# More expert blocks among the queries, and gathered rows begun four units later: a two-block transformer kernel on one core

## The chip, the cores and the metric

The kernel runs on 1 core of one Trainium2 chip. The metric is the device time of one execution in microseconds (us). Three runs of the kernel before gave 2555.89, 2561.6 and 2565.39 us (median 2561.6). One further execution was profiled; all rows below come from it.

## The reference

Two transformer blocks over 512 tokens of width 1024 in float32. The change touches only the feed-forward part of the first block, a "PEER" layer that retrieves 16 of 16384 single-neuron experts for each of 8 heads:

```
q = (xc @ wq).reshape(chunk, 8, 2, 128)
s = einsum('chpd,hpkd->chpk', q, subkeys)          # scores against 2 x 128 subkeys
s1, i1 = top_k(s[:, :, 0], 16); s2, i2 = top_k(s[:, :, 1], 16)
cand = s1[..., :, None] + s2[..., None, :]         # 16 x 16 candidates
cs, ci = top_k(cand, 16); eidx = experts of ci; g = softmax(cs)
hid = einsum('cd,chkd->chk', xc, u_table[eidx])
a   = gelu(hid) * g
out = einsum('chk,chkd->cd', a, v_table[eidx])
```

Ahead of it stand the attention heads of the first block, behind it the whole second block (retention, convolution, gated feed-forward); neither is changed.

## The kernel before, in words

**Two ways to the same experts.** For the first 384 tokens (`GT`) the kernel does not gather: it multiplies all 16384 experts densely, 128 blocks of 128 experts, and spreads the retrieved weights into a dense table `gates`. For the last 128 tokens it gathers the 128 retrieved rows of `u_table` and then those of `v_table` by indirect DMA (`row`, 128 x 1024 floats, 0.524 MB each, 256 in all) and multiplies them on VectorE (`gather_step`: `scr`/`hg` for the u rows, `acc` for the v rows).

**Units.** The dense work is a list `self.order` of units. A "q" unit is one 128-column chunk of the query projection, a "u" unit the up-projection of one expert block (`up`, 24 matmuls, then a gelu into `gel`), a "v" unit the down-projection of one block (18 matmuls into the six banks `oacc`). Every unit needs one weight tile of 0.524 MB: loaded into `ws` four units ahead (`DEEP`) by SyncE's DMA queue, rounded to a high part `wh` on ScalarE two units ahead (`AHEAD`, `stage_high`), and its low part `wl = ws - wh` made two units ahead as well (`stage_low`), on VectorE or GpSimd. TensorE multiplies high x high, high x low and low x high. A v unit also needs `gel` times its gates (`stage_gate`, VectorE), the high part `ah` of that (ScalarE) and its low part `al` (`stage_al`, VectorE).

**Three stages.** `run_queries`: q units, with u units dealt between them. VectorE meanwhile takes the top 16 of each score chunk (`tv`, `ti`); after every fourth chunk, a group of two heads, it forms the candidates (`cand` on VectorE, `cidx` on GpSimd), their top 16 (`cv`, `ci`) and, in pieces dealt between the next group's top-16s, the expert numbers (`oh`, `ov`, `ef`). The stage's result is `iff`, the indices as floats. `run_gates`: TensorE transposes the indices (`it`) and multiplies one-hot tables (`o`) into `gates`, again with u units between; each finished 2 MB part of `gates` is written to DRAM by a DMA on ScalarE's queue. `run_experts`: the other u units and all v units alternate; after the last u, v units alone. `weight` deals the 256 gathered rows over this stage's units.

**What sets the order.** These stages are recorded by hand: each engine runs its instructions in the order in which the code emits them. `plan` makes the list of units from estimated costs (`V_TOP`, `V_OH`, ...: VectorE's time of each piece, `PE_U`, `PE_Q`: TensorE's): it puts u units after a q unit while the estimated backlog of VectorE (`wait`) is over `BACK`. A u block done before there is room keeps its gelu in DRAM and is read back later (`gel<-gel_d`). In `run_queries` every fourth low part and the last five are on VectorE, the others on GpSimd, and each is emitted at the head of its unit:

```
pool = s < self.nq - 5 and s % 4 < 3
self.stage_low(x, self.nc.gpsimd if pool else self.nc.vector)
x = self.at(s + 1) if s + 1 >= 0 else None
if x is not None and x["k"] == "v":
    self.stage_al(x)
```

In `run_experts` the order within a unit is: load, `wh`, gate and `ah`; the gather steps; then `lows`, that is the low part `wl` two units ahead and, last, `al` one unit ahead; then the unit's matmuls. `NROW = 6` row buffers are in flight.

Of the kernel before, what the change touches and what calls it, by code (L numbers as in the profile page):

```python
# [22 lines left out]
NTB = 4  # L23
# [17 lines left out]
NROW = 6  # L41
AHEAD = 2
DEEP = AHEAD + 2
USTEP = 1.6
NQ = 3

PE_Q, PE_U, PE_GP, PE_IT = 6.35, 4.17, 0.95, 2.1
V_TOP, V_CAND, V_TOPC, V_OH, V_OV, V_RED, V_Z, V_LOW, V_O, V_PREP = 1.68, 5.0, 1.3, 0.6, 0.9, 0.9, 0.8, 1.25, 2.85, 4.5
BACK = 8.0
CAND = [(a, 16 // (a + 1)) for a in range(16)]  # L50
NCAND = sum(n for _, n in CAND)
# [43 lines left out]
class Builder:  # L95
# [384 lines left out]
    def plan(self):  # L480

        self.order, self.events = [], []
        un, wait = 0, NQ * NTB * V_TOP
        for c in range(NQ, 16):
            self.order.append({"k": "q", "c": c})
            wait += NTB * V_TOP - PE_Q
            if c % 4 == 3:
                wait += V_CAND + 8 * (V_TOPC + V_OH + V_RED) + V_Z + (4 * V_OV if c == 15 else 0)  # L490
            while wait > (BACK if c < 15 else 0):
                self.order.append({"k": "u", "i": un})
                wait -= PE_U
                un += 1
        self.nq = len(self.order)
        pt, dt = 0.0, V_PREP

        def fill(t):
            nonlocal pt, dt, un
            while pt < t():  # L500
                self.events.append(("u", 0))
                self.order.append({"k": "u", "i": un})
                pt, dt, un = pt + PE_U, dt + V_LOW, un + 1

        fill(lambda: dt)
        self.events.append(("it", 0))
        pt += PE_IT
        dt = max(dt, pt + 1.5)
        for i in range(GT // 8):
            dt += V_O  # L510
            fill(lambda: dt)
            self.events.append(("gp", i))
            pt += PE_GP
        self.ng = len(self.order)
        self.far = far = un - (LEAD - ME - AHEAD - 1)
        units = []
        for j in range(-ME, 128):
            while un < 128 + far and un - far < min(128, j + LEAD - AHEAD - 1):
                i = un
                un += 1  # L520
                units.append({"k": "u" if i < 128 else "re", "i": i, "j": i - far})
                if i < 128:
                    break
            if j >= 0:
                units.append({"k": "v", "j": j})
        for x in self.order:
            if x["k"] == "u":
                x["j"] = x["i"] - far if x["i"] >= far else 128 - far + x["i"]
        for x in units:
            if x["k"] == "re":  # L530
                self.order[-1].setdefault("re", []).append(x)
            else:
                self.order.append(x)
# [121 lines left out]

    def run_queries(self, ps):

        self.sk, self.qc, self.tvs = {}, {}, {}
        self.todo, self.pieces = deque(), deque()
        for c in range(NQ):  # L660
            self.load_sk(c)
        for s in range(-DEEP, 0):
            self.ahead(s)
            self.lows(s)
        for c, p in enumerate(ps):
            self.take_q(c, p)
        for c in range(NQ - 1):
            self.scores(c)
        pt = dt = 0.0
        old = NQ - 1  # L670
        for s in range(self.nq):
            x = self.order[s]
            self.ahead(s)
            self.lows(s)
            if x["k"] == "q":
                p = self.mm("q")
                self.mul(p, x)
                self.take_q(x["c"], p)
                pt += PE_Q
            else:  # L680
                self.stage_up(x)
                self.stage_gelu(x)
                pt += PE_U
            if old is not None:
                self.scores(old)
            old = x["c"] if x["k"] == "q" else None
            while self.todo and (dt < pt or s == self.nq - 1):
                cost, f = self.todo.popleft()
                f()
                dt += cost  # L690
            if not self.todo:
                dt = max(dt, pt)

# [10 lines left out]
    def run_gates(self):  # L704

        nc = self.nc
# [15 lines left out]
        def turn():  # L722
            for j in range(3):
                p = self.bank("at", "it")
                for tb in range(ND):
                    src = iff[:, j, tb] if j < 2 else self.g[:, tb].rearrange("p h k -> p (h k)")
                    nc.tensor.transpose(p[:, tb * 128:tb * 128 + 128], src, self.ident)
                if j < 2:
                    nc.scalar.activation(iT[j], p[:, :GT], AF.Copy)
                else:  # L730
                    nc.scalar.activation(gT[0], p[:, :GT], AF.Copy, scale=GSCALE)
                    nc.vector.scalar_tensor_tensor(gT[1], p[:, :GT], GSCALE, gT[0], op0=OP.mult, op1=OP.subtract)

        def hots(i):
            if i >= GT // 8:
                return
            t0 = 8 * i
            o = os[i] = [self.tmp.tile([128, 4, 128, 2], FP16, tag=f"o{j}", bufs=1 if j == 1 else 3, name=f"o{j}")
                         for j in range(4)]
            io = self.iota2[:, None].to_broadcast([128, 4, 128, 2])  # L740

            def bc(x):
                x = x[:, t0:t0 + 8].rearrange("p (j s) -> p j s", s=2)
                return x[:, :, None, :].to_broadcast([128, 4, 128, 2])

            nc.vector.tensor_tensor(o[0], io, bc(iT[0]), OP.is_equal)
            nc.vector.tensor_tensor(o[1], io, bc(iT[1]), OP.is_equal)
            nc.vector.tensor_tensor(o[2], o[1], bc(gT[0]), OP.mult)
            nc.vector.tensor_tensor(o[3], o[1], bc(gT[1]), OP.mult)
# [14 lines left out]
            if q == GC // 8 - 1:  # L764
                nc.scalar.dma_start(self.gd[:, c], gs[0])

        s = self.nq
        for kind, i in self.events:
            if kind == "it":
                turn()  # L770
                hots(0)
                hots(1)
            elif kind == "gp":
                spread(i)
                hots(i + 2)
            else:
                x = self.order[s]
                self.ahead(s)
                self.lows(s)
                self.stage_up(x)  # L780
                self.stage_gelu(x)
                s += 1

    def ahead(self, s):

        x = self.at(s + DEEP)
        if x is not None:
            self.stage_load(x)
        x = self.at(s + AHEAD) if s + AHEAD >= 0 else None
        if x is not None:  # L790
            self.stage_high(x)
            if x["k"] == "v":
                self.stage_gate(x)

    def lows(self, s):

        x = self.at(s + AHEAD) if s + AHEAD >= 0 else None
        if x is not None:
            pool = s < self.nq - 5 and s % 4 < 3
            self.stage_low(x, self.nc.gpsimd if pool else self.nc.vector)  # L800
        x = self.at(s + 1) if s + 1 >= 0 else None
        if x is not None and x["k"] == "v":
            self.stage_al(x)

    def wtile(self, tag, dt):

# [69 lines left out]
    def run_experts(self):  # L876


        self.grs, self.wcount = {}, {}
        self.load_gates(0)  # L880
        weight = [USTEP if x["k"] == "u" else 1.0 for x in self.order]
        n = len(self.order)
        total, spent, done, issued, last = sum(weight[self.ng:]), 0.0, 0, 0, []
        for s in range(self.ng, n):
            self.ahead(s)
            spent += weight[s]
            while done < (256 if s == n - 1 else min(256, 256 * spent / total)):
                while issued < min(256, done + NROW):
                    self.issue_row(issued)
                    issued += 1  # L890
                self.gather_step(done)
                done += 1
            self.lows(s)
            x = self.order[s]
            if x["k"] == "u":
                self.stage_up(x)
                self.stage_gelu(x)
            else:
                y = (x["j"], x["ah"], x["al"], x["wh"], x["wl"])
                if x["j"] < 128 - VT:  # L900
                    for i in range(6):
                        self.vmul(i // 2, i % 2, *y)
                else:
                    last.append(y)
        return last
# [442 lines left out]
```

## Time and profile before

| | |
|---|---|
| median of 3 runs | 2561.6 us (2555.89 to 2565.39) |
| the profiled execution | 2559.39 us, its span 2557.6 us |
| TensorE busy | 2471.1 us (97%) |
| VectorE / ScalarE / GpSimd busy | 1721.6 / 940.7 / 601.5 us |
| DMA over the span | 494.24 MB, mean 193 GB/s |

The span is what the profiler saw from the first to the last instruction; the execution takes 1.8 us more. Busy shares are means over stages with different limits, so each stage has to be read by itself. In a row of a timeline the bracket at the end is the idle time of that engine just before the instruction, and what ended it. PE is TensorE, DVE VectorE, ACT ScalarE, POOL GpSimd, SP SyncE; "q" behind a name is its DMA queue.

### The profile page before, as it was taken

What the parts mean: (1) busy time and instruction counts of PE and PEld (TensorE: products, weight loads), DVE (VectorE), ACT (ScalarE), POOL (GpSimd) and SP (SyncE); (2) the same over time, 40 slices, a digit from 0 to 9 for tenths busy, and PEclk for the clock granted to TensorE, in tenths of its full rate; (3) what the DMA queues carried; (4) which work ended last, traced back from release to release, by engine and by line L of the source; (5) the groups of instructions that cost most, each with busy time, mean ns of one, the idle gap of its engine ahead of it and who ended that gap; (6) DMA issues with size and microseconds to landing.
All of it is one profiled execution on the core that took longest, in us unless ns stands there. A gap on an engine that the chain in (4) does not pass through costs nothing.

```text
span 2557.6 us, 34104 instructions
## 1 busy us (share of the span) xinstructions
PE 2471.1 (97%) x12867; PEld 2138.2 (84%) x12867; DVE 1721.6 (67%) x3226; ACT 940.7 (37%) x1401; POOL 601.5 (24%) x455
## 2 busy tenths in 40 slices
PE   8999999997998999999999999999999999999998
PEld 6788898887997899999988787777888888888887
DVE  5767568999896788888887897777644335433323
ACT  4666343343553333333333333521232223422221
POOL 1132146541003455545443351100000001000000
PEclk9999999998998999999999999999999999999999
DMA  4476244334768999999999995422222223222332
GB/s 154 143 246 218 71 132 136 117 127 135 285 238 309 357 339 340 327 337 340 333 362 361 346 377 175 161 80 86 83 99 99 93 97 108 75 95 95 95 99 62
DMA packets 188693, 494.24 MB, mean 193 GB/s; under 512 B 15848, under 2 KB 83304, under 8 KB 186992
## 3 DMA queue, kind: packets, MB, share of 16 engines
q1 hardware_dynamic: 140768, 320.64, 37.2%
q0 software_dynamic: 36864, 134.23, 14.5%
q10 hardware_dynamic: 10896, 37.18, 3.9%
q8 instruction: 101, 1.65, 0.3%
q14 instruction: 64, 0.52, 0.1%
HBM read 454.10 MB, written 37.90 MB: 192 GB/s over the span
## 4 chain that ended last, share of the span: by engine, by line
PE 75%; DVE 12%; DMA 6%; ACT 3%; issue 3%; POOL 1%; SPq 0%; ACTq 0%; DVEq 0%; POOLq 0%
PE up L146 5%; PE up L148 5%; PE up L147 5%; DMA ws<-in_v_blk 5%; PE oacc L914 4%; PE oacc L913 4%; PE oacc L912 4%; PE fg L147 2%; PE fg L148 2%; PE fg L146 2%; PE fd L146 2%; PE fd L147 2%; PE fd L148 2%; PE fu L147 1%; PE fu L148 1%
## 5 line engine op out<-in xcount | busy, mean ns | idle before, releaser
L140 ACT ACTIVATE wh<-ws 128x1024 fp32r<-128x1024 f32 (+1 forms) x204 | 214.3, 1051 | 664.4 <-issue 233.7
L141 DVE TENSOR_TENSOR wl<-ws,wh 128x1024 fp32r<-128x1024 f32 (+1 forms) x198 | 240.5, 1215 | 255.0 <-ACT wh L140 253.6
L840 DVE TENSOR_TENSOR wl<-ws,wh 128x1024 fp32r<-128x1024 f32 x236 | 290.6, 1232 | 163.4 <-ACT wh L836 158.8
L836 ACT ACTIVATE wh<-ws 128x1024 fp32r<-128x1024 f32 x269 | 284.1, 1056 | 206.4 <-DMA ws<-in_v_blk 132.3
L148 PE MATMUL up<-xh,wl 128*128 128x384 f32 x1024 | 346.1, 338 | 12.4 <-DVE wl L840 11.7
L146 PE MATMUL up<-xh,wh 128*128 128x384 f32 x1024 | 348.2, 340 | 0.0
L147 PE MATMUL up<-xl,wh 128*128 128x384 f32 x1024 | 344.3, 336 | 0.0
L914 PE MATMUL oacc<-wh,al 128*128 128x512 f32 x768 | 302.7, 394 | 9.9 <-DVE al L856 9.8
L913 PE MATMUL oacc<-wl,ah 128*128 128x512 f32 x768 | 300.9, 392 | 0.0
L912 PE MATMUL oacc<-wh,ah 128*128 128x512 f32 x768 | 299.9, 390 | 0.0
L918 POOL DMA_INDIRECT row<-in_peer_u,eidx x128 | 179.8, 1405 | 359.7 <-ACT gst L762 186.8
L918 POOL DMA_INDIRECT row<-in_peer_v,eidx x128 | 188.1, 1470 | 232.8 <-DVE acc L944 208.0
L870 ACT ACTIVATE gel<-up 128x384 f32<-128x384 f32 x128 | 62.9, 492 | 433.2 <-PE up L148 433.1
L148 PEld LDWEIGHTS up<-xh,wl 128*128 128x128 f32 x1024 | 193.4, 189 | 15.7 <-DVE wl L840 12.9
L146 PEld LDWEIGHTS up<-xh,wh 128*128 128x128 f32 x1024 | 193.8, 189 | 2.1
L147 PEld LDWEIGHTS up<-xl,wh 128*128 128x128 f32 x1024 | 193.7, 189 | 2.1
L914 PEld LDWEIGHTS oacc<-wh,al 128*128 128x128 f32 x768 | 144.5, 188 | 45.6 <-DVE al L856 16.1
L933 DVE CUSTOM_DVE_ANT_0 scr<-row,xt 128x1024 bf16<-128x1024 f32 x128 | 156.4, 1222 | 19.4 <-DMA gates_d<-gst 15.3
L913 PEld LDWEIGHTS oacc<-wl,ah 128*128 128x128 f32 x768 | 144.5, 188 | 29.1
L912 PEld LDWEIGHTS oacc<-wh,ah 128*128 128x128 f32 x768 | 144.7, 188 | 28.1
L944 DVE SCALAR_TENSOR_TENSOR acc<-row,wg,acc 128x1024 f32<-128x1024 f32 x127 | 162.7, 1281 | 0.9
L141 POOL TENSOR_TENSOR wl<-ws,wh 128x1024 fp32r<-128x1024 f32 x6 | 14.4, 2400 | 571.3 <-ACT wh L140 571.3
(372 smaller groups left out, 5316.9 us busy)
## 6 DMA issues: line engine op xcount, KB each, us to landing
ws<-in_u_blk SPq DMA_DIRECT2D x128, 512.0 KB, 4.6
ws<-in_v_blk SPq DMA_DIRECT2D x128, 512.0 KB, 7.6
ws<-in_w_t SPq DMA_DIRECT2D x64, 512.0 KB, 3.3
ws<-in_ada_w SPq DMA_DIRECT2D x48, 512.0 KB, 4.4
gates_d<-gst ACTq DMA_DIRECT2D x12, 2048.0 KB, 7.2
gr<-gates_d SPq DMA_DIRECT2D x32, 768.0 KB, 10.0
ws<-in_ffn_gate SPq DMA_DIRECT2D x22, 512.0 KB, 3.3
ws<-in_ffn_up SPq DMA_DIRECT2D x22, 512.0 KB, 3.2
```

Of the source, the lines that this page charges most:

```text
L140: nc.scalar.activation(wh, ws, AF.Copy)
L141: (low or nc.vector).tensor_tensor(wl, ws, f32(wh), OP.subtract)
L146: mm(out, lhsT=wh, rhs=xh, start=first, stop=False)
L147: mm(out, lhsT=wh, rhs=xl, start=False, stop=False)
L148: mm(out, lhsT=wl, rhs=xh, start=False, stop=last)
L836: self.nc.scalar.activation(x["wh"], x["ws"], AF.Copy)
L840: eng.tensor_tensor(x["wl"], x["ws"], f32(x["wh"]), OP.subtract)
L912: mm(o, lhsT=ah[:, t], rhs=vh[:, d], start=j == 0, stop=False)
L913: mm(o, lhsT=ah[:, t], rhs=vl[:, d], start=False, stop=False)
L914: mm(o, lhsT=al[:, t], rhs=vh[:, d], start=False, stop=j == 127)
L918: self.nc.gpsimd.indirect_dma_start(out=u, out_offset=None, in_=self.a["peer_v" if i >= 128 else "peer_u"], in_offset=bass.IndirectOffsetO ...
L944: nc.vector.scalar_tensor_tensor(self.acc, u, self.wg[:, j:j + 1], self.acc, op0=OP.mult, op1=OP.add)
```

## The change

The planner's costs are corrected (`V_OH`, `V_OV`, `V_RED` up, and a quarter of a low part per unit is now counted), so that 40 u units stand among the queries where 34 stood, and 53 in the last stage where 59 stood; the 35 among the gates stay. There are 10 u units ahead of query chunk 4 before and 11 now, 17 and 20 ahead of chunk 8, 25 and 28 ahead of chunk 12, 25 and 29 ahead of chunk 15, 9 and 11 behind it. The low parts that VectorE makes in the query stage move behind about 2 us of top-k work of their unit, those in the gate stage behind the next one-hot tables. In the last stage `al` moves from the end of the unit to its head, the first gather step comes with the fifth unit instead of the first, and the rows are dealt by new weights: from 256 x 1.6/222.4 = 1.84 per u unit and 1.15 per v unit to 1.97 per u and 1.46 per v while both alternate, and 1.12 per v at the end.

```diff
-USTEP = 1.6
+LATE = 4
+STEP = {"u": 1.75, "v": 1.3, "last": 1.0}
...
-V_TOP, V_CAND, V_TOPC, V_OH, V_OV, V_RED, V_Z, V_LOW, V_O, V_PREP = 1.68, 5.0, 1.3, 0.6, 0.9, 0.9, 0.8, 1.25, 2.85, 4.5
+V_TOP, V_CAND, V_TOPC, V_OH, V_OV, V_RED, V_Z, V_LOW, V_O, V_PREP = 1.68, 5.0, 1.3, 0.7, 1.3, 0.95, 0.8, 1.25, 2.85, 4.5
...
-            wait += NTB * V_TOP - PE_Q
+            wait += NTB * V_TOP + V_LOW / 4 - PE_Q
...
-                wait -= PE_U
+                wait += V_LOW / 4 - PE_U
...
         for s in range(-DEEP, 0):
             self.ahead(s)
-            self.lows(s)
+            self.low_part(s, nc.gpsimd)
...
             self.ahead(s)
-            self.lows(s)
+            pool = s < self.nq - 5 and s % 4 < 3
+            if pool:
+                self.low_part(s, nc.gpsimd)
...
+            after = dt + 2.0 if self.todo else dt
             while self.todo and (dt < pt or s == self.nq - 1):
+                if not pool and dt >= after:
+                    pool = True
+                    self.low_part(s, nc.vector)
+                    dt += V_LOW
                 cost, f = self.todo.popleft()
                 f()
                 dt += cost
+            if not pool:
+                self.low_part(s, nc.vector)
+                dt += V_LOW
...
             elif kind == "gp":
                 spread(i)
                 hots(i + 2)
+                if low is not None:
+                    self.low_part(low, nc.vector)
+                    low = None
             else:
+                if low is not None:
+                    self.low_part(low, nc.vector)
                 x = self.order[s]
                 self.ahead(s)
-                self.lows(s)
+                low = s
...
-    def lows(self, s):
-
+    def low_part(self, s, eng):
         x = self.at(s + AHEAD) if s + AHEAD >= 0 else None
         if x is not None:
-            pool = s < self.nq - 5 and s % 4 < 3
-            self.stage_low(x, self.nc.gpsimd if pool else self.nc.vector)
-        x = self.at(s + 1) if s + 1 >= 0 else None
-        if x is not None and x["k"] == "v":
-            self.stage_al(x)
+            self.stage_low(x, eng)
...
-        weight = [USTEP if x["k"] == "u" else 1.0 for x in self.order]
-        n = len(self.order)
+        n, only = len(self.order), max(i for i, x in enumerate(self.order) if x["k"] == "u")
+        weight = [0.0 if i < self.ng + LATE else STEP["last" if i > only else x["k"]]
+                  for i, x in enumerate(self.order) if "k" in x]
         total, spent, done, issued, last = sum(weight[self.ng:]), 0.0, 0, 0, []
         for s in range(self.ng, n):
+            x = self.at(s + 1)
+            if x is not None and x["k"] == "v":
+                self.stage_al(x)
             self.ahead(s)
...
-            self.lows(s)
+            self.low_part(s, self.nc.vector)
```

Three places where this moves instructions on VectorE. First the candidates of the second group of chunks (`cand` is the sum, `cv` and `ci` the top 16 of it and its places), before:

```order
L606 TENSOR_TENSOR cand<-tv 128x8 x8
L697 MAX cv<-cand 128x8
L698 MAX_INDEX ci<-cv,cand 128x8
L700 MATCH_REPLACE rest<-cv,cand 128x50
L701 MAX cv<-rest 128x8
L702 MAX_INDEX ci<-cv,rest 128x8
L697 MAX cv<-cand 128x8
```

and now, from inside the second of these top-16s on:

```order
L710 MAX_INDEX ci<-cv,cand 128x8
L712 MATCH_REPLACE rest<-cv,cand 128x50
L713 MAX cv<-rest 128x8
L714 MAX_INDEX ci<-cv,rest 128x8
L854 TENSOR_TENSOR wl<-ws,wh 128x1024
L709 MAX cv<-cand 128x8
```

Before, eight top-16s follow the candidates without a break; now a low part stands behind the second. It is that of query chunk 8, which GpSimd made before, behind `cidx`. In the third group that of chunk 12 stands right behind `cand`, ahead of the top-16s.

Second the hand-over from the queries to the gates (`iff` are the indices that TensorE waits for, `gT` and `o` the one-hot tables), before:

```order
L717 CAST iff<-iu 128x768
L840 TENSOR_TENSOR wl<-ws,wh 128x1024 x2
L732 SCALAR_TENSOR_TENSOR gT_5894<-it,gT_5893 128x384
L746 TENSOR_TENSOR o_5979<-iota_5879,iT_5891 128x1024
L747 TENSOR_TENSOR o_5980<-iota_5879,iT_5892 128x1024
```

and now:

```order
L729 CAST iff<-iu 128x768
L854 TENSOR_TENSOR wl<-ws,wh 128x1024
L744 SCALAR_TENSOR_TENSOR gT_6098<-it,gT_6097 128x384
L758 TENSOR_TENSOR o_6181<-iota_6083,iT_6095 128x1024
L759 TENSOR_TENSOR o_6182<-iota_6083,iT_6096 128x1024
L760 TENSOR_TENSOR o_6183<-o_6182,gT_6097 128x1024
L761 TENSOR_TENSOR o_6184<-o_6182,gT_6098 128x1024
L758 TENSOR_TENSOR o_6189<-iota_6083,iT_6095 128x1024
L759 TENSOR_TENSOR o_6190<-iota_6083,iT_6096 128x1024
L760 TENSOR_TENSOR o_6191<-o_6190,gT_6097 128x1024
L761 TENSOR_TENSOR o_6192<-o_6190,gT_6098 128x1024
L854 TENSOR_TENSOR wl<-ws,wh 128x1024 x2
```

The second low part, that of the second u unit behind the transposes, has moved behind `gT` and eight one-hot tables.

Third the begin of the last stage (`scr` and `hg` are a gather step of a u row, `gel<-gel,gr` is a gate), before:

```order
L840 TENSOR_TENSOR wl<-ws,wh 128x1024 x2
L933 ISA scr,hg<-row,xt 128x1024
L933 ISA hg 128x1
L933 ISA scr,hg<-row,xt 128x1024
L933 ISA hg 128x1
L840 TENSOR_TENSOR wl<-ws,wh 128x1024
L933 ISA scr,hg<-row,xt 128x1024
L933 ISA hg 128x1
```

and now:

```order
L854 TENSOR_TENSOR wl<-ws,wh 128x1024 x6
L861 TENSOR_TENSOR gel<-gel,gr 128x384
L951 ISA scr,hg<-row,xt 128x1024
L951 ISA hg 128x1
L951 ISA scr,hg<-row,xt 128x1024
L951 ISA hg 128x1
L854 TENSOR_TENSOR wl<-ws,wh 128x1024
L870 TENSOR_TENSOR al<-gel,ah 128x384
L951 ISA scr,hg<-row,xt 128x1024
```

Before, two gather steps stood ahead of the low part of the stage's third unit. Now the low parts up to the sixth unit stand ahead of the first gather step, and two rows ahead of that of the seventh, the first v unit.

## Rows read from the trace of the kernel before

**Rows 1.** Windows by stage: length; busy PE, PEld, DVE, ACT, POOL; clock; DMA share; GB/s.

```profile
331.35:600.64 269.29, 241.98 (x1291) 224.26 (x1289) 234.11 (x938) 100.37 (x142) 138.73 (x125) 0.96 0.39 123
600.64:787.20 186.56, 186.56 (x1569) 181.18 (x1570) 162.17 (x228) 99.93 (x163) 3.81 (x4) 0.99 0.68 241
787.20:835.20 48.00, 37.48 (x191) 35.69 (x189) 27.49 (x40) 12.27 (x19) 22.88 (x18) 0.86 0.96 362
835.20:1268.75 433.55, 432.25 (x2185) 393.11 (x2185) 358.21 (x482) 146.73 (x211) 220.05 (x155) 1.00 0.95 340
1268.75:1575.30 306.55, 300.45 (x1312) 244.63 (x1312) 259.30 (x306) 111.80 (x149) 121.18 (x80) 1.00 0.96 343
```

**Rows 2.** Waits of PE, whole span: engine line <- releaser: total, times, longest us.

```profile
PE it L727 <- DVE iff L717: 17.0, 1, 17.0
PE up L148 <- DVE wl L840: 11.7, 4, 8.1
PE oacc L914 <- DVE al L856: 9.8, 9, 2.5
...
PE q L148 <- POOL wl L840: 5.8, 2, 3.4
```

**Rows 3.** Timeline of PE: first matmuls of a u, the next v, the next u.

```profile
857.50 0.33 PE L146 MATMUL up<-xh,wh 128*128 128x384 f32 x1
...
861.68 0.39 PE L912 MATMUL oacc<-wh,ah 128*128 128x512 f32 x1
...
865.80 0.33 PE L146 MATMUL up<-xh,wh 128*128 128x384 f32 x1
```

**Rows 4.** Timeline of PE: the transposes behind the queries.

```profile
600.64 1.54 PE L727 MATMUL it<-ident,iff 128*128 128x128 f32 x6 [16.99 <-DVE iff L717]
```

**Rows 5.** Timeline of DVE: the last group's first low part and first top-16.

```profile
518.86 1.23 DVE L840 TENSOR_TENSOR wl<-ws,wh 128x1024 fp32r<-128x1024 f32 x1 [2.76 <-ACT wh L836]
520.00 0.29 DVE L697 MAX8 tv<-sc 128x8 f32<-128x128 f32 x1
```

**Rows 6.** Window of the last group, columns as in rows 1.

```profile
520.00:600.00 80.00, 60.60 (x330) 57.39 (x328) 77.07 (x263) 26.49 (x37) 36.72 (x34) 0.90 0.33 106
```

**Rows 7.** Timelines of DVE, then POOL: candidates of the second group.

```profile
434.36 9.63 DVE L606 TENSOR_TENSOR cand<-tv 128x128 f32<-128x128 f32 x16
...
436.88 7.00 POOL L840 TENSOR_TENSOR wl<-ws,wh 128x1024 fp32r<-128x1024 f32 x3
```

**Rows 8.** Timelines of DVE, ACT's and SP's queues: begin of the last stage.

```profile
800.49 1.23 DVE L933 CUSTOM_DVE_ANT_0 scr<-row,xt 128x1024 bf16<-128x1024 f32 x1 [15.32 <-DMA gates_d<-gst]
...
802.91 1.22 DVE L840 TENSOR_TENSOR wl<-ws,wh 128x1024 fp32r<-128x1024 f32 x1
...
788.76 0.33 ACTq L765 DMA_DIRECT2D gates_d<-gst  x1
...
800.41 0.62 SPq L817 DMA_DIRECT2D gr<-gates_d  x1
```

**Rows 9.** DMA issues, whole span: KB each, median us to landing.

```profile
gates_d<-gst ACTq DMA_DIRECT2D x12, 2048.0 KB, 7.2
```

**Rows 10.** DMA issues of 787:835, columns as in rows 9.

```profile
ws<-in_u_blk SPq DMA_DIRECT2D x6, 512.0 KB, 10.5
...
ws<-in_v_blk SPq DMA_DIRECT2D x4, 512.0 KB, 16.1
```

**Rows 11.** Windows of the v units alone, columns as in rows 1.

```profile
1490.00:1538.00 48.00, 48.00 (x213) 39.41 (x212) 44.67 (x54) 19.86 (x26) 27.42 (x16) 1.00 1.04 383
...
1282.00:1490.00 208.00, 201.90 (x878) 163.49 (x877) 169.72 (x202) 72.10 (x96) 81.97 (x56) 1.00 1.00 357
```

**Rows 12.** Window, gather steps of u rows alone (L933): busy DVE; clock; DMA; GB/s.

```profile
835.20:1268.75 433.55, 138.87 (x226) 1.00 0.95 340
```

**Rows 13.** Waits of SP's DMA queue in 1268:1500, columns as in rows 2.

```profile
SPq L832 <- DVE al L856: 152.2, 47, 12.2
```

**Rows 14.** DMA issues of 835:1268, gathered rows of u: median us to landing.

```profile
row<-in_peer_u,eidx POOLq DMA_INDIRECT x107, 7.2
```

More of the change, by code (lines that the diff above doesn't have):

```diff
@@ L656, in run_queries @@
     def run_queries(self, ps):
+        nc = self.nc
         self.sk, self.qc, self.tvs = {}, {}, {}
@@ L765, in spread @@
                 nc.scalar.dma_start(self.gd[:, c], gs[0])
-        s = self.nq
+        s, low = self.nq, None
         for kind, i in self.events:
@@ L782, in run_gates @@
                 s += 1
+        if low is not None:
+            self.low_part(low, nc.vector)
     def ahead(self, s):
```

## The prediction

> **What bounds the kernel now.** I read the windows by stage first, then TensorE's waits, then the timelines around them. TensorE is busy without a break in the gate stage and in the stretch where u and v units alternate; it loses time in three places only: in the query stage (269.29 us, 241.98 busy, mean clock 0.96), at the begin of the last stage (48.00 us, 37.48 busy, clock 0.86) and where v units run alone (306.55 us, 300.45 busy) [rows 1]. The reader is to see in the waits what ends each loss: `iff` of VectorE 17.0 us, low parts 11.7 and 5.8, `al` 9.8 [rows 2]. A u unit costs TensorE 861.68 - 857.50 = 4.18 us, a v unit 865.80 - 861.68 = 4.12, a pair 8.30 [rows 3]. The change takes no matmul away, so all it can win are these losses, some 27 + 15 + 6 us, and all it can lose are new waits.
>
> **1. Queries.** TensorE runs out at 600.64 - 16.99 = 583.65 us and waits for VectorE's chain [rows 4]. Six u units more, 6 x 4.18 = 25.1 us, move ahead of that wait. If VectorE's end stood still, this stage would end at 600.64 as before while the last stage lost 25.1 us of work; but VectorE is fed by TensorE. Its last group starts at 520.00, as soon as chunk 12's scores are there (it had idled 2.76 us just before) [rows 5], and then it is busy 77.07 of 80 us [rows 6]: 600.64 - 520.00 = 80.6 us, a fixed chain. Two more low parts fall into it (eight instead of six), 520.00 - 518.86 = 1.14 us each [rows 5]: 83. So `iff` comes 83 us after chunk 12's scores, and these come three u units later, 12.5 us, less what TensorE waits less before them. Of the 5.8 us for GpSimd's low parts [rows 2] the longer wait, 3.4, is chunk 8's and should go, with its dip of the clock: VectorE's `cand` took 9.63 us there while GpSimd ran three low parts in a row for 7.00 us [rows 7]; now chunk 8's low part is VectorE's own, two top-16s behind `cand`, and eight u units instead of six give it time. Chunk 12's low part is now also VectorE's, behind `cand`, and I expect a new wait of some 3.5 us and a dip of the clock there. Nothing regained and this wait on top: scores 16 us later, `iff` at 619, gain 25.1 - 18.4 = 6.7. All waits gone: scores 3 us later, gain 20. I take `iff` at 610, 9.5 later: gain 15.6. TensorE then still waits some 9 us for it. From this goes a new wait: the low part of the second u unit behind the transposes now follows `gT` and eight tables. From `iff` to its end these are 1.14 + 9 x 0.71 + 1.14 = 8.7 us (0.71 is that stage's mean, 162.17/228 [rows 1]); TensorE needs it after the transposes (1.54 for six of nine [rows 4], so about 2) and one unit of 4.2: some 2.5 us. **Net -13** (bounds -4 and -20).
>
> The two low parts are the smaller half of what GpSimd adds: by the plan it makes 38 low parts in this stage instead of 33, at 7.00/3 = 2.33 us [rows 7]. The row of `cand` shows VectorE held for about as long as GpSimd's low parts ran. The Trainium skill says why in "SBUF — State Buffer", section "SBUF: two separate sides": VectorE instructions with two SBUF inputs and GpSimd's share one port pair that the first comer holds for its whole instruction. By that rule all five could land on the chain, 5 x 2.33 = 11.7 us; the row agrees for `cand`, but most of the chain (top-16s) reads one tensor, so I leave it to the bounds.
>
> **2. Begin of the last stage.** From 787.20 TensorE has six u, one v and one u to do, 33.4 us, and takes 48.0 [rows 1]; the next v waits 1.3 more: 16 lost. VectorE stood 15.32 us before its first gather step until 800.49, released by the last write of `gates`, and the third unit's low part, queued behind two such steps, came at 802.91 [rows 8]. With the steps four units later this low part waits for nothing, and TensorE can run units 1 to 4 until 787.2 + 16.7 = 803.9. Unit 5 is next: its `ws` stands on SyncE's queue behind the read of `gates`, which must wait for the last write. That write was issued at 788.76 and landed by 800.41 [rows 8], with rows in flight beside it; alone it takes 7.2 [rows 9], so about 796. A `ws` load in this crowd takes 10.5 us [rows 10], less now since five of the six first rows start only after that write: 7 to 10.5, then `wh` and `wl`, some 2 us by the 1.14 of the latter [rows 5]: 806 to 809, 2 to 5 us late. The two gather steps that come back with unit 5 stand only ahead of unit 7's low part, which TensorE needs six units in, at 812 or later. **Net -12** (bounds -4, if all loads take the v blocks' 16.1 us [rows 10], and -15).
>
> **3. Alternating units.** 47 pairs instead of 53. A pair moves two blocks, 2.99 rows and 0.197 MB of `gates`: 2.81 MB in 8.30 us is 339 GB/s, the window says 340 [rows 1]. Now 3.43 rows: 3.04 MB, 366 GB/s. The v stretch shows 383 GB/s over 48 us without a TensorE wait, and 357 over 208 us with some [rows 11]. VectorE is busy 358.21/433.55 x 8.30 = 6.86 us a pair [rows 1]; 0.43 gather steps of 138.87/113 = 1.23 us [rows 12] (each has two instructions) make it 7.39, under 8.30. Hidden, then; if the transfers stopped at 357 a pair would take 8.52, 47 x 0.22 = 10 us. **Net +1** (bounds 0 and +10).
>
> Here a rule speaks against the change. "DMA: Bandwidth & Descriptors" of the Trainium skill, section "Specifications", gives about 358 GB/s as HBM's limit for one core; by it a pair would take 8.50 us, +9 in all. This trace disagrees for a core alone: 383 [rows 11]. I keep it as a rival.
>
> **4. v units alone.** 6 us are lost to `al` [rows 1, 2]. A loop feeds them: SyncE's queue waits 152.2 us for `al` to free a gelu buffer [rows 13] and holds the next `ws` behind it, `wl` waits for that `ws`, and `al` stood behind `wl`. Now `al` stands at the head of its unit, some 3 us earlier, and `wl` has a unit to spare. There are six more of these v units, with 1.12 rows instead of 1.15. **Net -5** (bounds -6 and +1, the same loss over 8% more units).
>
> **Sum.** -13 - 12 + 1 - 5 = -29 on the profiled 2559.4 us gives 2530.4; this execution lies 2.2 below the median of the runs, so I predict 2533 us. Late next: still `iff`, then unit 5's load.
>
> **Rivals.**
> A. VectorE's chain slides with the added blocks (GpSimd's low parts hold it, or waits stay): term 1 is -4 instead of -13, 2542. For it: VectorE idles right before its group [rows 5], so a later score is a later end. Against: the waits it would need are those that the order removes.
> B. The transfers stop at 357 GB/s: term 3 is +10, term 4 is 0, 2547. For it 208 us at 357, against it 383 [rows 11].
> C. No wait for `iff` is left, term 1 is -20: 2526. It needs chunk 12's scores 6 us earlier than I think; nothing shows that.
> D. The begin keeps its burst (loads at 16.1 us) and the new low-part order costs what the six blocks bring: terms 1 and 2 near -4 together, 2554, no change. For it: units 5 to 8 still wait on loads behind `gates` [rows 8].
> E. Slower: the rows bind the alternating stretch. Six buffers and 3.43 rows in 8.30 us allow 14.5 us from one issue to the next of a buffer; a landing of 7.2 [rows 14] and a step of 1.23 leave room, and it decides from a landing of about 13. At the 16.1 us that blocks took in the crowd [rows 10] a round is 17.3, a pair 9.9 and 47 of them +75: 2533 - 1 + 75 = 2607. Against it: TensorE is full there with 2.99 rows a pair [rows 1], and 7.2 is little over half of 13.
>
> **Chances.** Forecast 0.52 (own range 2520 to 2544), A 0.15, B 0.08, C 0.08, D 0.12, E 0.05. A change of 0.5%, 12.8 us, is about what a measurement of this kernel tells from none: faster is under 2548.8, slower over 2574.4. Faster takes the forecast, A, C, most of B: 0.80; D and the rest make 0.14 the same; E with a little beside it 0.06 slower. The range reaches to C's far side and past D: 2514 to 2556.
>
> **What would show it.** Term 1: a wait for `iff` of 5 to 13 us at about 610 instead of 17 at 600.6, no wait of chunk 8 for GpSimd, a short one at chunk 12, and 2 to 3 us for a low part after the transposes. Term 2: VectorE not idle for `gates`, TensorE's clock up, one wait of 2 to 5 us at unit 5. Term 3: over 360 GB/s and TensorE still full. Term 4: few waits for `al`. I am wrong if `iff` comes after 618, if the alternating stretch shows waits for low parts behind rows, or if the begin still loses 10 us.

## The result, and the profile after

The changed kernel takes 2521.41 us (median; 2520.87 to 2522.66) against 2563.49 of the kernel before in the same comparison: ratio 0.9843, 95% interval 0.983 to 0.9855. Its profiled execution took 2520.87 us, 38.5 less than the profiled one before, with a span of 2518.6.

Windows by stage, after (columns and stages as in [rows 1]: queries, gates, begin of the last stage, alternating units, v units alone):

```profile
332.28:607.61 275.33, 260.09 (x1436) 245.68 (x1434) 227.29 (x940) 110.55 (x154) 154.07 (x129) 0.98 0.43 137
607.61:796.90 189.29, 187.68 (x1569) 181.99 (x1570) 161.63 (x228) 99.96 (x163) 1.13 (x1) 0.99 0.65 236
796.90:832.30 35.40, 33.93 (x191) 32.54 (x189) 18.73 (x26) 11.35 (x18) 14.07 (x12) 1.00 0.90 339
832.30:1214.40 382.10, 382.10 (x1934) 347.92 (x1934) 343.07 (x469) 131.43 (x187) 230.53 (x159) 1.00 1.00 375
1214.40:1535.60 321.20, 321.20 (x1418) 265.89 (x1418) 277.66 (x327) 117.61 (x160) 108.22 (x85) 1.00 0.98 352
```

In the last three windows TensorE was idle for 10.5, 1.3 and 6.1 us before [rows 1]; now for 1.5 in the first of them and not at all in the other two, and its granted clock is full in all three (0.86, 1.00 and 1.00 before). The first two are 8.8 us longer than before and hold six u units more (25.1 us). Waits of TensorE over the whole span, after (as [rows 2]; `oacc <- al` and the queries' wait for GpSimd's `wl` no longer stand in the list):

```profile
PE it L739 <- DVE iff L729: 11.5, 1, 11.5
...
PE up L149 <- DVE wl L854: 4.0, 4, 1.6
...
PE up L149 <- POOL wl L854: 1.5, 2, 1.4
...
PE up L147 <- ACT gel L884: 1.2, 1, 1.2
```

Timeline of TensorE at the transposes and one u unit behind them (as [rows 4]), then VectorE's candidates of the second group and first top-16 of the last one (as [rows 7, 5]):

```profile
607.61 1.54 PE L739 MATMUL it<-ident,iff 128*128 128x128 f32 x6 [11.54 <-DVE iff L729]
...
617.36 0.44 PE L149 MATMUL up<-xh,wl 128*128 128x384 f32 x1 [1.61 <-DVE wl L854]
```

```profile
442.85 2.40 DVE L607 TENSOR_TENSOR cand<-tv 128x128 f32<-128x128 f32 x16
...
523.14 0.29 DVE L709 MAX8 tv<-sc 128x8 f32<-128x128 f32 x1 [4.40 <-ACT sc L572]
```

The chain from that top-16 to `iff` takes 607.61 - 523.14 = 84.5 us (83 predicted); it starts 3.1 us later and ends 7.0 later than before; 0.9 of each lies ahead of the stage. `cand` takes 2.40 us instead of 9.63.

Timelines of VectorE, ScalarE's and SyncE's queues at the begin of the last stage, after (as [rows 8]):

```profile
802.82 1.23 DVE L854 TENSOR_TENSOR wl<-ws,wh 128x1024 fp32r<-128x1024 f32 x1 [4.49 <-ACT wh L850]
814.61 1.22 DVE L854 TENSOR_TENSOR wl<-ws,wh 128x1024 fp32r<-128x1024 f32 x1 [10.56 <-ACT wh L850]
```

```profile
798.46 0.33 ACTq L777 DMA_DIRECT2D gates_d<-gst  x1
```

```profile
804.84 0.63 SPq L831 DMA_DIRECT2D gr<-gates_d  x1
```

VectorE no longer stands before a gather step for the write of `gates`; the read behind that write goes out 7.9 us after the stage's start (13.2 before). Unit 5's load, behind that read, costs TensorE 1.5 us: its high part starts on ScalarE only at 813.52, and the gelu that frees unit 5's `up` buffer stands behind it (1.2, the wait for `gel` in the list); its low part, at 814.61, costs the other 0.3.

### The profile page after: what moved, and what is told of

Its sections match the earlier page's. It is cut to its first block, busy times and chain, and to the rows that moved or that the text cites. A ratio compares the mean times of both kernels' runs of the same rounds, so it can differ in the third digit from the quotient of the medians.

```text
span 2518.6 us, 34208 instructions
## 1 busy us (share of the span) xinstructions
PE 2460.0 (98%) x12867; PEld 2135.6 (85%) x12867; DVE 1707.9 (68%) x3221; ACT 940.9 (37%) x1401; POOL 604.8 (24%) x460
## 3 DMA queue, kind: packets, MB, share of 16 engines
q0 software_dynamic: 36864, 134.23, 14.1%
## 4 chain that ended last, share of the span: by engine, by line
PE 90%; DVE 6%; ACT 2%; DMA 1%; issue 1%; POOL 0%; ACTq 0%; SPq 0%; DVEq 0%; POOLq 0%
PE oacc L931 7%; PE oacc L932 7%; PE oacc L930 7%; PE up L149 6%; PE up L147 6%; PE up L148 6%; PE fg L148 2%; PE fg L149 2%; PE fg L147 2%; PE fd L147 2%; PE fd L149 2%; PE fd L148 2%; PE fu L147 2%; PE fu L148 2%; PE fu L149 2%; PE o L415 1%
## 5 line engine op out<-in xcount | busy, mean ns | idle before, releaser
L142 DVE TENSOR_TENSOR wl<-ws,wh 128x1024 fp32r<-128x1024 f32 (+1 forms) x198 | 240.5, 1214 | 254.0 <-ACT wh L141 252.6
L854 DVE TENSOR_TENSOR wl<-ws,wh 128x1024 fp32r<-128x1024 f32 x231 | 284.2, 1231 | 108.3 <-ACT wh L850 105.9
L936 POOL DMA_INDIRECT row<-in_peer_v,eidx x128 | 172.5, 1348 | 233.8 <-DVE acc L962 213.4
```

What stands on the lines that cost most here:

```text
L142: (low or nc.vector).tensor_tensor(wl, ws, f32(wh), OP.subtract)
L854: eng.tensor_tensor(x["wl"], x["ws"], f32(x["wh"]), OP.subtract)
L936: self.nc.gpsimd.indirect_dma_start(out=u, out_offset=None, in_=self.a["peer_v" if i >= 128 else "peer_u"], in_offset=bass.IndirectOffsetO ...
```

## The experiments

Each was timed in the same runs as the kernel before. To say where a kernel loses, its last stage was cut at the same matmuls in each trace, and the time of full units taken off: 4.18 us for each of the six u units at the begin, 8.30 a pair, and for the v units alone 321.2 us for 81 (75: 296.8; 84: 333.5), in each case without their last 41 matmuls, which run among later work. That is 321.2/1417 matmuls x 18 = 4.08 us for a v unit behind a v unit, a little less than the 4.12 between two u units [rows 3]. "Queries" goes from the last transpose of the tokens (`xt`, the stage's first work on TensorE, at 321.8 to 327.3 us in these traces) to the transposes of the indices. Columns with no other unit are in us; each trace is one execution. Kernels with the same query stage show how far to trust that column: after, e1, e2, e4, e10 and e13 lie from 282.9 to 283.0, but before, e5 and e6 from 274.1 to 276.9. TensorE's last `xt`, before and after:

```profile
323.72 0.27 PE L546 MATMUL xt<-ident,y 128*128 128x128 f32 x1
```

```profile
324.65 0.28 PE L547 MATMUL xt<-ident,y 128*128 128x128 f32 x1
```

| kernel | ratio to before (95%) | rows per v unit alone | u among queries | queries | gates | lost: begin | alternating | v alone |
|---|---|---|---|---|---|---|---|---|
| before | 1 | 1.15 | 34 | 276.9 | 186.6 | 10.3 | 6.2 | 9.6 |
| after | 0.9843 (0.983-0.9855) | 1.12 | 40 | 283.0 | 189.3 | 2.0 | 0.3 | 0 |
| e1 | 0.9874 (0.9855-0.9893) | 1.09 | 40 | 283.0 | 189.3 | 9.0 | 0.3 | 0 |
| e2 | 0.9878 (0.9857-0.99) | 1.12 | 40 | 283.0 | 190.8 | 1.6 | 2.8 | 2.7 |
| e3 | 0.9869 (0.9851-0.9886) | 1.07 | 34 | 264.8 | 189.3 | 1.3 | 1.9 | 0 |
| e4 | 0.9849 (0.9828-0.9871) | 1.24 | 40 | 283.0 | 189.3 | 1.6 | 0.3 | 0 |
| e5 | 0.9953 (0.9938-0.9968) | 1.19 | 34 | 274.5 | 187.7 | 0.6 | 5.2 | 16.4 |
| e6 | 0.9923 (0.9904-0.9942) | 1.15 | 34 | 274.1 | 187.0 | 10.8 | 0.6 | 0 |
| e7 | 0.9945 (0.9926-0.9964) | 1.20 | 40 | 286.6 | 187.9 | 11.1 | 5.9 | 16.0 |
| e10 | 0.9946 (0.9925-0.9967) | 1.24 | 40 | 282.9 | 189.3 | 3.9 | 0.8 | 27.9 |
| e13 | 0.9926 (0.9907-0.9944) | 1.24 | 40 | 282.9 | 190.8 | 2.0 | 1.0 | 21.7 |
| e11 | 0.9814 (0.9791-0.9836) | 1.16 | 43 | 283.7 | 190.7 | 5.4 | 0.3 | 0 |
| e12 | 0.9799 (0.9778-0.982) | 1.16 | 43 | 286.2 | 186.0 | 4.8 | 0.3 | 0 |
| e14 | 0.9789 (0.9774-0.9803) | 1.16 | 43 | 286.3 | 186.0 | 0 | 5.7 | 0 |

My first theory was the prediction's: gains that add up, one for each part. The rival each time: another part made the gain.

**e1: rows begun at once.**

```
-LATE = 4
+LATE = 0
```

> The changed kernel (2521) with LATE = 0: gathered rows start with the first unit of the last stage again, all else as changed. Theory: rows and gather steps at the stage's first units made the loss at its begin (14.6 + 1.9 us there before, 2.0 after), so 14 us come back: 2535, with VectorE idle for the write of gates and a dip of TensorE's clock at 797 to 830. Rival: the loss went because al no longer stands behind the low part and six units fewer follow, so the place of the rows does not matter: 2521 +- 3.

Measured 2526.38 us. Waits of TensorE from 790 to 1545 us, and VectorE's first gather step there:

```profile
PE up L149 <- DVE wl L854: 6.3, 1, 6.3
```

```profile
805.56 1.22 DVE L951 CUSTOM_DVE_ANT_0 scr<-row,xt 128x1024 bf16<-128x1024 f32 x1 [13.52 <-DMA gates_d<-gst]
```

VectorE's stand for `gates` and the low part behind it are back, but only 7 us of the 14 at the begin: half of the theory's loss.

**e2: `al` behind the low part again**, all else as changed.

```
-            x = self.at(s + 1); ... self.stage_al(x)
             self.ahead(s)
...
             self.low_part(s, self.nc.vector)
+            x = self.at(s + 1); ... self.stage_al(x)
```

> The changed kernel with al emitted behind the low part of its unit, as before, all else as changed. Theory: the place of al alone cured the stretch of v units (9.7 us lost before, none after): 2531, with waits of TensorE for al there. Rival 1: the smaller share of rows (1.12 a v unit instead of 1.15) cured it: 2521 +- 3. Rival 2: with the heavier row share of the alternating units al waits there too: 2536 or more.

Measured 2527.98 us, but no wait for `al` over 0.3 us in the v units alone, which lose 2.7 us. The place of `al` is not the only cure there. Of some 9 us by the ratio (give or take 5), the last stage shows 5; 1.5 more stand in the gates, and 1.1 ahead of the queries, both of which this edit leaves alone.

**e3: the planner's old costs**, so 34 u units, with the new order of low parts.

```
-V_OH, V_OV, V_RED = 0.7, 1.3, 0.95      (and V_LOW / 4 charged per unit)
+V_OH, V_OV, V_RED = 0.6, 0.9, 0.9       (no charge)
```

> The changed kernel with the planner's old costs (VectorE's table pieces 0.6, 0.9 and 0.9 us, no charge for low parts), so 34 u units among the queries instead of 40; the order of low parts, rows and al as changed. Theory: the six units filled the wait for iff, so some 16 us come back: 2537, TensorE waiting 20 us or more for iff. Rival: the order of the low parts made half of that gain by taking away the waits for GpSimd's low parts and their dips of the clock; then scores and iff come earlier and only 8 us come back: 2529.

Measured 2526.76 us: near the rival's 8 us, not 16. VectorE's second-group candidates and last group's first top-16, then TensorE's transposes:

```profile
434.39 4.65 DVE L607 TENSOR_TENSOR cand<-tv 128x128 f32<-128x128 f32 x16
...
508.05 0.29 DVE L709 MAX8 tv<-sc 128x8 f32<-128x128 f32 x1 [2.82 <-ACT sc L572]
```

```profile
588.78 1.54 PE L739 MATMUL it<-ident,iff 128*128 128x128 f32 x6 [21.54 <-DVE iff L729]
```

Chunk 12's scores and `iff` come 12 us earlier than before with the same 34 units: the order of the low parts alone shortens the stage by 12.1 us, less 2.7 given back in the gates.

**e4: the old weights of rows**: `STEP = {"u": 1.6, "v": 1.0, "last": 1.0}`.

> The changed kernel with the old weights of rows (u 1.6, every v 1.0; gather still begun four units late): 1.24 rows a v unit in the stretch of v units instead of 1.12, 3.22 a pair instead of 3.43. Theory: rows are hidden in both stretches, 2521 +- 3. Rival: the share of rows in the last stretch counts, VectorE and the transfers are late there and al waits: 2526 to 2531.

Measured 2521.06 us: no loss at 1.24 rows a v unit. The four undone parts give back some 8, 9, 7 and 2 us by their ratios, each give or take 5: 25 of 40. So the parts seem to stand in for one another, and the next four runs look for it from the other side.

**e5: the kernel before with the late rows alone.**

```
-        weight = [USTEP if x["k"] == "u" else 1.0 for x in self.order]
+        weight = [0.0 if i < self.ng + LATE else USTEP if ... else 1.0 ...]
```

> The kernel before (2560) with one part of the change: no gather step and no row before unit 5 of the last stage (old weights from there on). Theory now, after the undone parts gave back less than the whole: the begin lost twice, 8 us to a low part behind the first gather steps and 6 us to the al of the first two v units; rows begun later take the first loss only: 2552, the waits for al stay at the first v units and in the stretch of v units. Rival: rows begun later cure the stretch of v units too, since all later steps stand otherwise: 2542.

Measured 2551.0 us, as the theory said. The begin is cured (10.3 to 0.6), the v units lose more than before. Waits of TensorE from 780 to 1575 us:

```profile
PE oacc L916 <- DVE al L857: 13.1, 12, 3.1
```

**e6: the kernel before with `al` first alone** (e2's lines, the other way).

> The kernel before (2560) with one part of the change: al at the head of its unit, ahead of the loads and gather steps, in the last stage. Theory: this alone takes away every wait for al, 6 us at the first two v units and 9.7 us in the stretch of v units: 2545, while the 8 us wait for a low part at the begin stays. Rival: the place of al is not what cured the stretch of v units (undoing it cost 3 us there, not 10): 2551 to 2554.

Measured 2543.53 us, 19.7 less: the first two v units' 5.6 us and the v units' 9.6 are gone, and from 780 to 1565 us TensorE has one wait left:

```profile
PE up L148 <- DVE wl L837: 8.4, 1, 8.4
```

**e7: the kernel before with the planner's new costs alone** (e3's lines, the other way).

> The kernel before (2560) with one part of the change: the planner's new costs, so 40 u units among the queries instead of 34, low parts placed as before. Theory: the six units alone give what they gave on top of the new order of low parts, 6 us, since half of their 25 us comes back as a later iff: 2554. Rival 1: they fill the whole old wait of 17 us: 2543. Rival 2: the old order of low parts holds VectorE's chain for the added blocks and iff slides by as much as is put ahead of it: 2560.

Measured 2546.89 us. Queries and gates: 25.1 - (286.6 - 276.9) - 1.3 = 14.1 us gained, nearer to rival 1's 17 than to 6, and 6.4 of it lost again in the v units, which now carry 1.20 rows. VectorE's second-group candidates, then TensorE's transposes:

```profile
438.81 3.76 DVE L606 TENSOR_TENSOR cand<-tv 128x128 f32<-128x128 f32 x16
```

```profile
609.61 1.54 PE L727 MATMUL it<-ident,iff 128*128 128x128 f32 x6 [7.87 <-DVE iff L717]
```

So the order alone shortens queries and gates by 9.4 us (e3), the six units alone by 14.1, both by 25.1 - 6.1 - 2.7 = 16.3, each against the trace of before; against e5's, 8.1, 12.8 and 15.0. (No run has the new order alone in the kernel before; e3 has it with the new last stage, and only its queries and gates are used here.) Much of it is one loss that both cure: TensorE's waits ahead of chunk 12's scores, mostly for GpSimd's low parts [rows 2], and the clock dips behind them. Windows from `xt` to these scores, of before, e3, e7 and after; the last two hold three u units (12.5 us) more:

```profile
323.72:517.46 193.74, 186.47 (x1011) 172.25 (x1010) 156.61 (x674) 76.24 (x108) 105.02 (x93) 0.98 0.41 130
```

```profile
323.97:506.33 182.36, 181.21 (x1011) 170.23 (x1010) 148.16 (x674) 76.15 (x107) 109.12 (x94) 1.00 0.43 139
```

```profile
323.04:522.60 199.56, 196.37 (x1083) 184.12 (x1082) 150.10 (x675) 82.70 (x116) 109.02 (x95) 0.99 0.43 138
```

```profile
324.65:521.40 196.75, 194.16 (x1083) 182.64 (x1082) 147.60 (x674) 82.68 (x116) 115.84 (x96) 1.00 0.45 140
```

Less the added units that is 11.4 us regained in e3, 6.7 in e7 and 9.5 with both: it can be won once. Both also part `cand` from GpSimd's three low parts (4.65 and 3.76 us instead of 9.63; 7.19 in e5 and e6, whose query stage is that of before). In the kernel before, one of `cand`'s small adds took 7.15 us, as long as those three low parts (7.00 [rows 7]), where the median add took 0.25 (ns, shortest/median/longest):

```profile
L606 DVE TENSOR_TENSOR cand<-tv x64: 160/251/7151, 361.4 to 564.1; 128x8 f32<-128x8 f32 x32, 128x16 f32<-128x16 f32 x12, 128x128 f32<-128x128 f32 x4, 128x64 f32<-128x64 f32 x4
```

That VectorE's loss there reached TensorE is not shown: behind it VectorE sat idle for 2.76 us until 456.38.

**e10: two parts of the last stage undone at once**, e2 and e4 together.

> The changed kernel (2521) with two parts undone at once: al behind the low part, and the old weights of rows (1.24 rows a v unit in the stretch of v units, more than the 1.15 of the kernel before). Theory: with al last the stretch of v units loses by the rows it carries (2.7 us at 1.12, 9.7 at 1.15 before), so 10 us or more come back there: 2535. Rival: the loss there came from the backlog that the kernel before took along from its begin, not from the rows: 2525 to 2528.

Measured 2547.99 us, some 26 more than after, where e4 alone costs nothing and e2 some 9. With `al` last, the loss of the v units rises with their rows: 2.7 us at 1.12, 9.6 at 1.15, 16.4 and 16.0 at 1.19 and 1.20, 27.9 at 1.24. With `al` first it is 0 from 1.07 to 1.24.

**e13: e10 with the gather steps behind the low part and `al`.**

> The kernel of e10 (2548: al behind the low part, 1.24 rows a v unit) with the gather steps moved behind the low part and al in each unit; the same rows, loads and instructions, and al still behind the low part. Theory: the stretch of v units loses because the gather steps (1.28 us each, one or two a unit) stand ahead of the low part and al, so al comes late, frees its gelu buffer late and holds the next loads on SyncE's queue: with the steps last the 28 us fall under 5, 2521 to 2525. Rival: the loads alone are late (al waits for the low part, this for its load), the place of the steps does not matter: the loss stays at 20 us or more, 2540 to 2548.

Measured 2546.59 us: my theory fell, 21.7 of the 27.9 us stay, as the rival said. Windows of 1220 to 1450 us, then the waits of SyncE's queue from 1220 to 1455; first e4 (`al` first), then e10, then e13, with the same rows a unit:

```profile
1220.00:1450.00 230.00, 230.00 (x1017) 190.50 (x1016) 203.12 (x241) 84.35 (x112) 119.94 (x71) 1.00 1.05 383
```

```profile
1220.00:1450.00 230.00, 211.46 (x913) 171.30 (x912) 182.50 (x214) 74.20 (x100) 104.25 (x63) 0.99 0.98 342
```

```profile
1220.00:1450.00 230.00, 217.53 (x929) 173.72 (x928) 185.08 (x219) 76.67 (x102) 83.59 (x64) 0.99 0.98 347
```

```profile
SPq L846 <- DVE al L870: 95.9, 37, 5.3
```

```profile
SPq L846 <- DVE al L870: 156.5, 50, 8.6
```

```profile
SPq L846 <- DVE al L870: 168.6, 52, 8.2
```

The transfers are no limit: 383 GB/s with `al` first, 342 and 347 with it last. The loop is load, high part, low part, `al`, gelu buffer free, next load. In e10, VectorE, then ScalarE:

```profile
1418.57 1.28 DVE L962 SCALAR_TENSOR_TENSOR acc<-row,wg,acc 128x1024 f32<-128x1024 f32 x1
1426.46 1.23 DVE L854 TENSOR_TENSOR wl<-ws,wh 128x1024 fp32r<-128x1024 f32 x1 [6.61 <-ACT wh L850]
1427.60 0.55 DVE L870 TENSOR_TENSOR al<-gel,ah 128x384 fp32r<-128x384 f32 x1
```

```profile
1425.37 1.06 ACT L850 ACTIVATE wh<-ws 128x1024 fp32r<-128x1024 f32 x1 [9.37 <-DMA ws<-in_v_blk]
```

`al` needs nothing of that load, yet stands behind its low part for 6.6 us. The loads do not land more slowly for it: from 1225 to 1450 us a load takes 9.5 us from issue to landing in the changed kernel, which loses nothing there, and 9.5 in e10 (medians; e4's trace shows no landings):

```profile
ws<-in_v_blk SPq DMA_DIRECT2D x58, 512.0 KB, 9.5
```

```profile
ws<-in_v_blk SPq DMA_DIRECT2D x49, 512.0 KB, 9.5
```

So what is late is their issue, not their landing. The queue's wait for `al` is no loss by itself: in the changed kernel it is 131.8 us from 1214 to 1446, and TensorE loses nothing. Why the loss rises with the rows is not shown.

**e11 and e12: more units.** TensorE still waits 11.5 us for `iff`. e11 puts three more u units behind chunk 15:

```
-            while wait > (BACK if c < 15 else 0):
+            while wait > (BACK if c < 15 else -12.0):
```

> The changed kernel (2521) with three more u units behind chunk 15's query (43 among the queries instead of 40), where they hold up no score. Theory: the chain from chunk 12's scores to iff is VectorE's alone, so iff stands still and the 12.5 us of units fill the 11.5 us that TensorE still waits for it, with its dip of the clock: 2509. Rival: their low parts push iff by as much as is put ahead of it, as half of the first six units' time came back so: 2515 to 2521.

e12 adds `BACK = 14.0`, and the low part of the second unit behind the transposes ahead of the tables:

```
                 turn()
+                if low is not None:
+                    self.low_part(low, nc.vector)
+                    low = None
                 hots(0)
```

> As e11, with two things more: the planner lets VectorE fall 14 us behind instead of 8, which moves units from ahead of chunks 4 and 15 to behind chunk 15, and the low part of the second u unit behind the transposes is issued ahead of the tables. Theory: scores of the first chunks come a unit (4.2 us) earlier and VectorE, which idles before them, with them, and the 1.6 us wait behind the transposes goes: 2505 if iff was still waited for, else 2508. Rival: VectorE has idle time later anyway, iff stays and only the 1.6 us goes: 2508 to 2510, which this run can't tell from the former; a time above e11's speaks against both.

e11 measured 2513.29 us: the wait for `iff` is gone, and the queries gain 12.5 - 0.8 = 11.7; the begin lost 3.4 and the gates 1.4 of it. e12 measured 2509.51 us, the version to keep: the gates gained 4.8, the wait of 2.8 us behind the transposes and a clock dip of 3.4 us with it. Waits of TensorE from 325 to 640 us, e11, then e12:

```profile
PE up L149 <- DVE wl L854: 5.0, 3, 2.8
...
PE it L739 <- ACT iT L741: 0.9, 1, 0.9
```

```profile
PE up L149 <- DVE wl L857: 3.7, 4, 1.2
...
PE it L739 <- ACT iT L741: 0.8, 1, 0.8
```

`BACK` lost 2.5 us in the queries (286.2 us against 283.7, and 286.3 again in e14). From `xt` VectorE makes `iff` 3.3 us earlier than in e11, as the theory wanted, but TensorE no longer waits for it and reaches the transposes later, with 5.7 us idle in the stage instead of 3.7, in waits for low parts. So e12 without `BACK` might be some 2.5 us faster (an estimate from these two columns; not run). VectorE's `iff`, e11 (`xt` at 325.36), then e12 (`xt` at 322.73):

```profile
608.13 0.56 DVE L729 CAST iff<-iu 128x768 f32<-128x768 uint32 x1
```

```profile
602.16 0.56 DVE L729 CAST iff<-iu 128x768 f32<-128x768 uint32 x1
```

**e14: e12 with unit 5's load ahead of the read of `gates`**: `load_gates(0)` behind the first `ahead(s)`.

> The kernel of e12 (2509.5) with the load of unit 5's block put ahead of the first read of gates on SyncE's queue at the begin of the last stage. Theory: TensorE's one wait there, 2.8 us for unit 5, stands behind that read, which must wait for the last write of gates; with the load ahead of it the wait goes: 2506 to 2507. Rival: the load waits for its buffer or lands late in the crowd anyway, or v0's gate is late instead: 2509 to 2511.

Measured 2509.66 us, no gain, the rival's. Waits of TensorE from 780 to 900 us, e12, then e14:

```profile
PE up L147 <- ACT gel L887: 2.8, 1, 2.8
```

```profile
PE up L147 <- ACT wh L853: 2.5, 1, 2.5
PE up L149 <- DVE wl L857: 0.6, 1, 0.6
```

Unit 5's wait is gone, so it did stand behind that read; the load of the second pair's u unit, issued in the same crowd at 808.06 and landed at 833.6, is late instead. Its issuing instruction alone took 11.54 us on SyncE's queue:

```profile
808.06 11.54 SPq L844 DMA_DIRECT2D ws<-in_u_blk  x1
```

## Why the prediction was right, and where not

**Sum.** 2533 was forecast, 2521.4 came, just inside the lower end of the forecast's own range (2520 to 2544): the mechanisms of terms 1, 2 and 4 came, each larger than forecast, term 4 mis-sized most. All three errors go the same way, so none made up for another. By the windows: queries and gates 8.8 - 25.1 = -16.3; begin -14.2 (10.3 + 6.2 lost before, 2.0 + 0.3 after); alternating 0; v units -9.6; and 0.9 lost ahead of the queries, where nothing was changed. That is -39 against the -38.5 of the two profiled executions.

**Term 1, -13 predicted, -16.3 measured** (-14 to -15 if e5 and e6, which share its query stage, stand for before). `iff` came at 607.6 (610 predicted), TensorE's wait was 11.5 us (9), the low part behind the transposes 1.6 (2.5). Chunk 8's wait for GpSimd went, as forecast. The wrong step is "a new wait of some 3.5 us" at chunk 12: none came, nor did the clock dip. "GpSimd's low parts hold" the chain (rival A) did not happen either: 84.5 us with 38 low parts in the stage. (VectorE's own low parts in the chain are nine instead of seven, where I had eight instead of six; two more either way.) What the term left out is that order and units are largely two cures of one loss (e3, e7); the forecast reckoned both in one chain and so did not suffer.

**Term 2, -12 predicted, -14.2 measured.** The 16 us lost before were read rightly, and unit 5 was the next to be late, by 1.5 us (2 to 5 predicted). But I gave all of it to the late rows. They took 7 to 10 (e1, e5); the other 6, at the first two v units, went with `al` (e6), which the prediction named only in term 4.

**Term 3, +1 predicted, 0 measured.** 375 GB/s and TensorE 382.10 of 382.10 us; VectorE 343.07/382.10 x 8.30 = 7.45 us a pair (7.39 predicted). Rivals B and E are out: weights old or new make no difference (e4). The limit of 358 GB/s that "DMA: Bandwidth & Descriptors" of the Trainium skill, section "Specifications", gives for one core does not hold for this core alone (375, and 383 in e4); "HBM Reference" of the Trainium skill, section "Specifications (TRN2)", says as much of a core that streams alone, and these runs agree.

**Term 4, -5 predicted, -9.6 measured.** The loop was the right one: e6 shows it alone. Mis-sized was the loss "6 us": window minus busy TensorE [rows 1]. A matmul is drawn 0.39 us long while the next starts 0.23 us after it, so the first 0.16 us of every wait show as busy, and held-up matmuls are drawn longer still. By the shortest full unit, 4.08 us, the stretch's 1309 matmuls at 321.2/1417 us are 296.8 of its 306.4 us, so 9.6 were lost. "Perfetto Trace Analysis" of the Trainium skill, section "Identifying the Most-Contended Engine", warns that matmul busy time misleads and points to the weight loads: these were busy 244.63 of 306.55 us before [rows 1] and 265.89 of 321.20 after. At the second share the first sum of loads takes 295.5 us, 11 less than 306.55, nearer to 9.6 than 6 is.

**Rivals.** C (2526, no wait left for `iff`) lies nearest in time, but its mechanism did not come: 11.5 us of wait stayed, which e11 then took. What D feared came only in part: the begin's loads still land in a crowd (medians of 797 to 840 us: 13.6 and 12.3 us for u and v blocks, 10.5 and 16.1 before [rows 10]), but they are issued 5 us earlier in the stage and TensorE waits 1.5 us for them; and the low parts' order gains.

## What to carry to other kernels

An operation that needs nothing of a load should not be queued behind one that does: its buffer then holds the next load, and here the loop lost the more, the more rows went beside it (2.7 to 27.9 us). Undo each part of a change, undo two at once, and make each alone: undone parts that give back 25 us of 40, and a pair that gives back 26 where its members give back 2 and 9, say that parts stand in for one another. Measure a loss by the shortest full unit, not by window minus busy time.

## What the runs showed of the hardware

TensorE's granted clock was at half (1.2 GHz) for 13.65 us around the wait for `iff` in the changed kernel, the first 5 us behind it included; in e11, where that wait is gone, for 3.41 us near there, behind a wait of 2.8 us. One core alone moved 383 GB/s for 230 us beside a full TensorE (e4). In a crowd of loads, rows and reads of `gates` a load of 0.5 MB landed 25 us after its issue began, 11.5 of them in the issuing instruction (e14: 808.06 to 833.6); over the alternating units of the changed kernel its median was 8. One add of VectorE took 7.15 us beside three instructions of GpSimd that ran in a row for 7.00 us; beside the same three, in e5 and e6, two adds took 2.4 us each, one GpSimd instruction long.
